# A planner that lets the accesses of all engines to one bank of products follow one another, reads too

## The chip, the cores and the metric

The kernel runs on one core of a Trainium2 chip. The core has a matmul engine (PE, with weight loads shown apart as PEld), a vector engine (DVE), an activation engine (ACT), GpSimd (POOL) and a queue that issues most transfers (SP). PE writes its products into eight banks of a memory of their own; DVE and ACT read them there. The metric is the device time of one execution in microseconds (us). The time before is the median of three runs: 1121.27 us (1120.59 to 1122.06).

## What is computed

One layer of a streaming encoder on 512 frames of 2048 features, all in float32:

```python
proj = einsum('btd,dc->btc', x, w_in)                  # 8320 columns
rw = token_shift(proj[..., :RWKV_COLS], shift_mu)      # y + mu * (y_prev - y)
o_rwkv = rwkv7_scan(...)                               # 16 heads of 64, gated with silu(z)
#   sa = S @ a_t;  S = S * w_t + sa b_t' + v_t k_t';  o_t = S @ r_t   for each frame
o_hgrn = hgrn2_chunkwise(...)                          # 8 heads of 128, gated
y = einsum('btc,cd->btd', concat([o_rwkv, o_hgrn]), w_out)
out = layer_norm(ALPHA * x + y) * ln_w + ln_b
```

## The kernel before, in words

**Projections.** Weights come in halves of 128 x 512 by `load` (SP, a ring of two tiles `wr`). `split` turns each into a rounded high part on ACT (`wh`, line 301) and a low part on DVE (`wl`, line 311); inputs are split in the same way into `xh` and `xl`. A product is then three wide matmuls of 512 columns (`three`, line 396). There are 65 blocks of 128 columns for the input projection, then the output projection in five column blocks. These wide matmuls fill a bank of the ring `main` (four banks); `shift`, `silu2` and `gates` drain it through ACT and DVE.

**Beside them** run the small works, as generators in queues: the preparation of a pair of RWKV heads (`rwkv_prep`), inversion and scan for two pairs at a time (`rwkv_group`, `rwkv_scan`), their end (`rwkv_finish`), and two HGRN heads at a time (`hgrn_heads`). There are four such groups, so four scan stretches. The scan goes chunk by chunk, eight chunks of 64 frames, and two pairs at once. In one chunk PE multiplies the state `bd` with `ar` into `px` (ring `acc`, two banks); DVE makes `rt` from it; PE makes `psa`; ACT or DVE copies that into `z`; PE multiplies `z` with `bt` into `pd` and puts the next chunk's share beside it in the same bank (ring `mix`, two banks). Out of `pd` DVE updates both halves of the state (line 320, `bd<-mix`), and the next `z` is copied (`z<-mix`, two halves of 64 x 64, ACT at line 301 or DVE at line 353). The other half of `px` is added to the output on DVE (line 311, `t<-t,acc`), which frees the bank.

**At the turn** from the input to the output projection, gated tiles that were put aside in DRAM (`put_gated`) come back through SP (`reload`, line 1184) and are split on ACT and DVE (`split_gated`). SP's queue holds them behind weight loads, and a weight load waits until the split of an older weight has freed its tile.

**Order.** Nothing is ordered by hand. While the kernel is built, a `Plan` keeps a clock for each engine. After each wide matmul, `pump` asks the head of each queue; `best` takes the engine on which the next operation would end first (a copy has a way on ACT and one on DVE), and `step` issues it if by the plan's clock its operands are there: PE only if they have been there for 0.35 us (`LEAD`), the others if they come within 0.5 us (`EARLY`). The start is worked out in `start` (line 79): each tile read must have been written (`seen`, which adds the hand-over `AFTER` from the writer's engine), and each tile written must be free of earlier accesses (`busy`), for PE only if the bank is newly taken. Two reads of one bank by two engines know nothing of one another there. On the chip each engine then works through its rows in the order in which they were issued, and waits on semaphores.

Of the kernel before, what the change touches and what calls it, by code (L numbers as in the profile page):

```python
# [56 lines left out]
class Plan:  # L57
# [11 lines left out]
    def __init__(self, room):  # L69
        self.clock = {"pe": 0.0, "dve": 0.0, "act": 0.0, "pool": 0.0, "dma": 0.0}  # L70
        self.table = None
        self.narrow = False
        self.queues = []
        self.ready, self.busy = {}, {}
        self.room = room
        self.slots = {tag: [(0, 0.0)] * n for tag, n in room.items()}
        self.count, self.used = 0, {}

    def start(self, e, op):

        t = 0.0
        for r in op.reads:
            t = max(t, self.seen(r, e))
        for w in op.writes:
            x, by = self.busy.get(w, (0.0, e))
            if e != "pe" or by is None:
                t = max(t, x if by == e else x + self.AFTER[by])
        return t

    def seen(self, name, e):  # L90

        x, by = self.ready.get(name, (-1.0, None))
        if by == e == "pe":
            return x
        return x + self.AFTER[by] + (self.TO_PE if e == "pe" else 0.0)
# [111 lines left out]
def mixer_kernel(ctx, tc, x_t, x_r, w_all, par, up, ln_wb, consts, hmask, out):  # L207
    nc = tc.nc
    pe, sc_e, dve, pool = nc.tensor, nc.scalar, nc.vector, nc.gpsimd
# [9 lines left out]
    def nm(s):  # L219
        uid[0] += 1  # L220
        return f"{s}{uid[0]}"
# [5 lines left out]
    plan = Plan({**BUFS, **PBUFS})  # L227
    tags = {}

    def st(tag, shape, dt=F32):  # L230
        return spool.tile(shape, dt, tag=tag, name=nm(tag), bufs=BUFS[tag])

    def take(tag, shape=(P, T), dt=F32):

        if not plan.free(tag):
            raise RuntimeError(f"no room: {tag}")
        slot = min(plan.slots[tag])
        plan.slots[tag].remove(slot)
        if tag in PBUFS:
            t = ppool.tile(list(shape), dt, tag=tag, name=nm(tag), bufs=PBUFS[tag])  # L240
        else:
            t = st(tag, list(shape), dt)
        name = t.tensor.name
        plan.busy[name] = (slot[1], None)
        tags[name] = tag
        return t
# [32 lines left out]
    def mm(o, l, r, start=True, stop=True, **kw):  # L279
        m, n = size(l), size(r)  # L280
        narrow = m < P or l.shape[0] < P
        if r.dtype == F32R:
            cost = n / 2400 + 0.0135
        elif narrow:
            cost = 0.025 if m <= 32 else 0.09 if m <= 64 else 0.16
        else:
            cost = n / 600 + 0.005
        return Op([("pe", cost, lambda: pe.matmul(o, l, r, start=start, stop=stop, **kw))], [l, r], [o],  # L288
                  narrow=narrow)
# [123 lines left out]
    def main_ps(tags=("main",)):  # L413

        def test():
            now = plan.clock["pe"]
            return [t for t in tags if plan.free(t) and min(plan.slots[t])[1] + 0.15 <= now]

        plan.until(test)
        return take(min(test(), key=lambda t: min(plan.slots[t])[1]))  # L420
# [110 lines left out]
    def shift(ps, col, put):  # L531
        def run():
            yield evac_room()
            t = take("t")
            yield act(t, ps, AF.Identity, scale=om[:, col : col + 1])
            yield stt(t[:, 1:], ps[:, : T - 1], pcol(PC_MU, col), t[:, 1:], ALU.mult, ALU.add)
            drop(ps)
            put(t)

        plan.add(evacs, run())  # L540
# [20 lines left out]
    def next_up():  # L561
        if len(ups) < NPAIR:
            upw = take("up", [P, 2, P])
            nc.sync.dma_start(upw, up[len(ups)])
            plan.fetched(upw, 8 * P)
            ups.append(upw)
# [810 lines left out]
    for b in range(4):  # L1377
        w = blocks[b][1]
# [88 lines left out]
```

## Time and profile before

| | |
|---|---|
| median of three runs | 1121.27 us |
| the profiled execution, its own time | 1123.09 us |
| its span, first to last instruction | 1121.3 us |
| granted TensorE clock, mean | 0.991 |
| last wide matmul starts | 1104.2 us |
| HBM read and written | 99.92 MB, 7.34 MB |

The span is what the trace covers. The scans stand in the stretches from about 140 to 220, 380 to 480, 580 to 660 and 830 to 930 us. The first output block begins at 916.6 us. A row of the timeline gives start, duration, engine, line, operation, the tiles written and read, and in brackets how long the engine was idle before it and who ended that.

### The profile page before, as it was taken

What the parts mean: (1) busy time and instruction counts of PE and PEld (TensorE: products, weight loads), DVE (VectorE), ACT (ScalarE), POOL (GpSimd) and SP (SyncE); (2) the same over time, 40 slices, a digit from 0 to 9 for tenths busy, and PEclk for the clock granted to TensorE, in tenths of its full rate; (3) what the DMA queues carried; (4) which work ended last, traced back from release to release, by engine and by line L of the source; (5) the groups of instructions that cost most, each with busy time, mean ns of one, the idle gap of its engine ahead of it and who ended that gap; (6) DMA issues with size and microseconds to landing.
All of it is one profiled execution on the core that took longest, in us unless ns stands there. A gap on an engine that the chain in (4) does not pass through costs nothing.

```text
span 1121.3 us, 19205 instructions
## 1 busy us (share of the span) xinstructions
PE 1091.5 (97%) x7402; PEld 901.8 (80%) x7402; DVE 766.5 (68%) x1739; ACT 456.3 (41%) x1042; POOL 88.6 (8%) x163
## 2 busy tenths in 40 slices
PE   8999999999999999999999999999999999999994
PEld 7878878788888878788887888888887778888893
DVE  6658967645579767857986774657976776624468
ACT  6532365433332465534245552433346444322221
POOL 0000000000010000101000010001000010000015
PEclk8999999999999999999999999999999999999997
DMA  7222211133323311223231122322231145433433
GB/s 274 85 80 93 95 59 58 57 99 94 90 75 103 96 58 59 67 79 117 76 104 58 58 76 87 99 92 77 94 102 46 52 141 194 136 122 110 144 126 138
DMA packets 36667, 108.50 MB, mean 97 GB/s; under 512 B 4320, under 2 KB 6496, under 8 KB 36448
## 3 DMA queue, kind: packets, MB, share of 16 engines
q1 hardware_dynamic: 34848, 104.33, 29.2%
q10 hardware_dynamic: 1728, 2.95, 0.7%
q8 instruction: 58, 0.95, 0.4%
q14 instruction: 33, 0.27, 0.1%
HBM read 99.92 MB, written 7.34 MB: 96 GB/s over the span
## 4 chain that ended last, share of the span: by engine, by line
PE 89%; DVE 6%; ACT 2%; issue 1%; DMA 1%; POOL 0%; SPq 0%; DVEq 0%; ACTq 0%
PE main L396 68%; PE mix L288 10%; PE mix L396 3%; PE acc L396 3%; PE acc L288 3%; PE mix L292 2%; DVE q L320 1%; DVE wl L311 1%; DVE t L311 1%; ACT z L301 1%; DVE bd L320 1%; ACT wh L301 1%; DMA t<-x_t 0%; DVE inv L320 0%; DMA t<-spill 0%
## 5 line engine op out<-in xcount | busy, mean ns | idle before, releaser
L396 PE MATMUL main<-xh,wh 128*128 128x512 f32 x896 | 358.0, 400 | 2.2 <-ACT xh L301 2.2
L396 PE MATMUL main<-xh,wl 128*128 128x512 f32 x896 | 356.6, 398 | 0.0
L396 PE MATMUL main<-xl,wh 128*128 128x512 f32 x896 | 356.0, 397 | 0.0
L301 ACT ACTIVATE wh<-wr 128x512 fp32r<-128x512 f32 (+1 forms) x313 | 195.5, 626 | 268.9 <-PE main L396 203.9
L311 DVE TENSOR_TENSOR wl<-wr,wh 128x512 fp32r<-128x512 f32 (+1 forms) x313 | 213.5, 683 | 130.2 <-ACT wh L301 126.9
L396 PEld LDWEIGHTS main<-xh,wh 128*128 128x128 f32 x896 | 169.1, 189 | 36.0 <-ACT xh L301 2.6
L396 PEld LDWEIGHTS main<-xl,wh 128*128 128x128 f32 x896 | 168.9, 188 | 33.8 <-DVE xl L311 0.8
L396 PEld LDWEIGHTS main<-xh,wl 128*128 128x128 f32 x896 | 168.9, 189 | 33.5
L396 PE MATMUL main<-wh,xh 128*128 128x512 f32 (+1 forms) x272 | 108.0, 397 | 1.9 <-DVE t L320 1.9
L396 PE MATMUL main<-wh,xl 128*128 128x512 f32 (+1 forms) x272 | 108.1, 397 | 0.0
L396 PE MATMUL main<-wl,xh 128*128 128x512 f32 (+1 forms) x272 | 107.4, 395 | 0.0
L301 ACT ACTIVATE z<-mix 64x64 f32<-64x64 f32 (+1 forms) x245 | 56.0, 229 | 92.1 <-DVE bd L320 71.4
L396 PEld LDWEIGHTS main<-wh,xh 128*128 128x128 f32 x272 | 51.3, 189 | 10.4 <-DVE t L320 2.3
L396 PEld LDWEIGHTS main<-wh,xl 128*128 128x128 f32 x272 | 51.3, 189 | 8.6
L396 PEld LDWEIGHTS main<-wl,xh 128*128 128x128 f32 x272 | 51.3, 189 | 8.2
L302 ACT ACTIVATE t<-main,om 128x512 f32<-128x512 f32 x33 | 22.6, 688 | 61.2 <-PE main L396 61.1
L320 DVE SCALAR_TENSOR_TENSOR bd<-mix,pc,bd 64x64 f32<-64x64 f32 x112 | 31.2, 283 | 22.4 <-PE mix L288 17.2
L343 POOL TENSOR_TENSOR rs<-rs,mhalf 128x8 f32<-128x8 f32 (+1 forms) x16 | 25.1, 1572 | 250.3 <-DVE rs L316 129.5
L311 DVE TENSOR_TENSOR inv<-inv 64x30 f32<-64x30 f32 (+14 forms) x120 | 38.6, 322 | 3.1
L311 DVE TENSOR_TENSOR inv<-inv,inv 64x30 f32<-64x30 f32 (+14 forms) x120 | 38.6, 322 | 2.9
L346 POOL MEMSET z<- 64x128 f32 x64 | 11.9, 199 | 355.7 <-PE acc L288 312.1
L311 DVE TENSOR_TENSOR t<-t,tot 128x256 f32<-128x256 f32 x96 | 38.4, 416 | 0.2
(207 smaller groups left out, 1489.1 us busy)
## 6 DMA issues: line engine op xcount, KB each, us to landing
wr<-w_all SPq DMA_DIRECT2D x158, 512.0 KB, 3.5
t<-x_t SPq DMA_DIRECT2D x16, 256.0 KB, 5.6
g<-x_r SPq DMA_DIRECT2D x16, 256.0 KB, 4.2
spill<-g SPq DMA_DIRECT2D x12, 256.0 KB, 4.3
t<-spill SPq DMA_DIRECT2D x12, 256.0 KB, 4.0
big<-ln_wb SPq DMA_DIRECT2D x1, 2048.0 KB, 9.1
out<-q ACTq DMA_DIRECT2D x7, 256.0 KB, 2.4
up<-up SPq DMA_DIRECT2D x8, 128.0 KB, 2.8
```

What stands on the lines that cost most here:

```text
L288: return Op([("pe", cost, lambda: pe.matmul(o, l, r, start=start, stop=stop, **kw))], [l, r], [o], narrow=narrow)
L292: return Op([("pe", 0.11, lambda: pe.transpose(o, i, ident))], [i], [o])
L301: return "act", cost, lambda: sc_e.activation(o, i, f, scale=scale)
L302: return "act", cost, lambda: sc_e.activation(o, i, f, scale=scale, bias=bias)
L311: return dve_op([a, b], o, lambda: dve.tensor_tensor(o, a, b, f), base=0.16 if o.shape[0] < P and size(o) == C and o.tensor.name in tags e ...
L320: return dve_op([a, b], o, lambda: dve.scalar_tensor_tensor(o, a, s, b, f1, f2), per=0.00113, base=0.085 if o.shape[0] == P else 0.25 if s ...
L343: lambda: pool.tensor_tensor(o, i, mhalf[:, : size(o)], ALU.pow))], [i], [o])
L346: return Op([("pool", 0.1, lambda: pool.memset(o, v))], [], [o])
L396: pe.matmul(ps, l, r, start=first and i == 0, stop=last and i == 2)
```

## The change

A tile from one of the rings of banks is entered in a set `banks`. A read of such a tile now also waits, in the plan, for the last access of any other engine to it, be it a write or a read (`done`). A write by PE now waits for another engine's last access to the bank; between PE's own accesses there is still no wait. Nothing else in the kernel changes: the same operations with the same shapes, their order and the choice between ACT and DVE being the plan's.

```diff
-        self.ready, self.busy = {}, {}
+        self.ready, self.busy, self.banks = {}, {}, set()
...
         for r in op.reads:
             t = max(t, self.seen(r, e))
+            if r in self.banks:
+                t = max(t, self.done(r, e))
         for w in op.writes:
-            x, by = self.busy.get(w, (0.0, e))
-            if e != "pe" or by is None:
-                t = max(t, x if by == e else x + self.AFTER[by])
+            t = max(t, self.done(w, e))
         return t
+
+    def done(self, name, e):
+
+        x, by = self.busy.get(name, (0.0, e))
+        return (0.0 if e == "pe" else x) if by == e else x + self.AFTER[by]
...
             t = ppool.tile(list(shape), dt, tag=tag, name=nm(tag), bufs=PBUFS[tag])
+            plan.banks.add(t.tensor.name)
```

What this moves, in two places. Line numbers after the change are 5 or 6 higher (L301 becomes L307, L311 L317, L320 L326, L353 L359).

*First place: the second scan stretch, a chunk in its middle.* `bd` is the state, `z` the next chunk's input, and both are read out of one bank (`mix_4269` of the one pair and `mix_4275` of the other before, `mix_4312` and `mix_4424` now). DVE before:

```order
L320 SCALAR_TENSOR_TENSOR bd_3736<-mix_4269,pc_3088,bd_3736 64x64
L320 SCALAR_TENSOR_TENSOR bd_3719<-mix_4275,pc_2695,bd_3719 64x64
L320 SCALAR_TENSOR_TENSOR bd_3736<-mix_4269,pc_3088,bd_3736 64x64
L311 TENSOR_TENSOR wl_4285<-wr_4103,wh_4284 128x512
L320 SCALAR_TENSOR_TENSOR bd_3719<-mix_4275,pc_2695,bd_3719 64x64
L311 TENSOR_TENSOR t_2762<-t_2762,acc_4222 64x64
```

DVE now:

```order
L326 SCALAR_TENSOR_TENSOR bd_3735<-mix_4312,pc_3088,bd_3735 64x64
L333 COPY_PREDICATED nr_3908<-hm,mix_4317 128x8x8
L333 COPY_PREDICATED nr_3909<-hm,mix_4317 128x8x8
L317 TENSOR_TENSOR t_3449<-t_3449,tot_3910 128x32x8
L326 SCALAR_TENSOR_TENSOR rt_3720<-acc_4307,z_3715 64x128
L326 SCALAR_TENSOR_TENSOR bd_3735<-mix_4312,pc_3088,bd_3735 64x64
L317 TENSOR_TENSOR wl_4359<-wr_4081,wh_4358 128x512
L359 COPY z_3732<-mix_4312 64x64 x2
```

ACT at the same place before:

```order
L301 ACTIVATE t_3160<-acc_4212 64x128
L301 ACTIVATE t_2762<-acc_4222 64x128
L301 ACTIVATE z_3733<-mix_4269 64x64 x2
L301 ACTIVATE wh_4284<-wr_4103 128x512
L301 ACTIVATE z_3713<-mix_4275 64x64 x2
L301 ACTIVATE bd_3718<-bd_3719,pc_2695 128x128
```

ACT now:

```order
L307 ACTIVATE wh_4407<-wr_4213 128x512
L307 ACTIVATE bd_3736<-bd_3735,pc_3088 128x128
L307 ACTIVATE z_3730<-mix_4416 64x128
L307 ACTIVATE z_3731<-mix_4416 64x128
L307 ACTIVATE bt_3733<-mix_4416 128x128
L307 ACTIVATE t_3160<-acc_4402 64x128
L307 ACTIVATE z_3732<-mix_4436 64x64 x2
L307 ACTIVATE z_3713<-mix_4424 64x64
```

The copy of `z` from the bank of the one pair has gone from ACT to DVE, behind DVE's own two reads of that bank; of the other pair's copy one half stays on ACT, later in its queue. The two chunks no longer interleave as tightly.

*Second place: the turn to the output projection, on DVE.* `xl` is the low part of the first reloaded tile. Before, from the split that frees the tile for SP's next weight load:

```order
L311 TENSOR_TENSOR wl_9119<-wr_8893,wh_9118 128x512
L353 COPY z_8255<-mix_9133 64x64 x2
L317 TENSOR_SCALAR sm_9041<-sm_9041 128x8
L353 COPY t_9025<-nr_8430 32x4x32
L320 SCALAR_TENSOR_TENSOR t_9147<-main_8911,pr,t_9147 128x511
L311 TENSOR_TENSOR wl_9160<-wr_9005,wh_9159 128x512
L311 TENSOR_TENSOR t_7683<-t_7683,acc_9107 64x64 x2
L311 TENSOR_TENSOR t_7287<-t_7287,sm_9041 128x512
L311 TENSOR_TENSOR xl_9178<-t_9138,xh_9177 128x512
```

Now the same split (`wl_9086`) stands seven rows above the first of these:

```order
L317 TENSOR_TENSOR t_7972<-t_7972,tot_8433 128x8x32
L317 TENSOR_TENSOR t_8068<-t_8068,tot_8433 128x8x32
L317 TENSOR_TENSOR tot_8434<-tot_8433 128x8
L317 TENSOR_TENSOR t_8182<-t_8182,tot_8435 128x8x32
L317 TENSOR_TENSOR t_8404<-t_8404,tot_8435 128x8x32
L317 TENSOR_TENSOR t_7287<-t_7287,acc_9076 64x64
L317 TENSOR_TENSOR tot_8436<-tot_8435 128x8
L317 TENSOR_TENSOR wl_9157<-wr_9018,wh_9156 128x512
L317 TENSOR_TENSOR t_7287<-t_7287,acc_9076 64x64
L326 SCALAR_TENSOR_TENSOR bd_8258<-mix_9188,pc_7611,bd_8258 64x64
L330 TENSOR_REDUCE sm_9173<-t_7287 128x8
L317 TENSOR_TENSOR xl_9199<-t_9108,xh_9198 128x512
```

Seventeen rows instead of seven lie between the two; HGRN rows (`tot`) that came later before now stand here, and the last scan chunk still runs here. In the whole program the wide matmuls keep their order; the scans end up to 35 wide matmuls later in each stretch, and 53 instructions go from ACT to DVE.

## The prediction

> **What bounds the kernel now.** I read the head of the page first, then the table of busy time by stretches, then the starts on PE one by one, then the waits.
>
> ```profile
> span 1121.3 us, 19205 instructions
> PE 1091.5 (97%) x7402; PEld 901.8 (80%) x7402; DVE 766.5 (68%) x1739; ACT 456.3 (41%) x1042; POOL 88.6 (8%) x163
> ```
>
> PE holds 97% of the span and nobody else comes near, so the time is PE's work plus the moments in which PE starts late. The change leaves PE's 7402 matmuls as they are. What it can win or lose is lateness, and the table by stretches says where that is:
>
> ```profile
> 140.00:220.00 80.00, 78.16 (x882) 63.99 (x872) 56.63 (x186) 45.18 (x146) 4.94 (x13) 1.00 0.17 55
> 220.00:380.00 160.00, 160.00 (x836) 131.30 (x835) 106.95 (x199) 56.70 (x95) 11.26 (x20) 1.00 0.30 94
> 380.00:480.00 100.00, 97.86 (x934) 79.38 (x933) 75.55 (x219) 53.60 (x159) 6.37 (x15) 1.00 0.21 66
> 480.00:580.00 100.00, 100.00 (x492) 82.64 (x491) 78.48 (x153) 35.68 (x61) 7.81 (x18) 1.00 0.31 93
> 580.00:660.00 80.00, 78.78 (x874) 64.54 (x873) 54.49 (x175) 42.84 (x140) 6.38 (x13) 1.00 0.21 65
> 660.00:830.00 170.00, 169.99 (x893) 139.20 (x892) 113.04 (x218) 60.78 (x104) 11.25 (x20) 1.00 0.30 91
> 830.00:930.00 100.00, 95.35 (x887) 77.13 (x886) 71.83 (x209) 52.02 (x155) 7.39 (x14) 1.00 0.27 85
> 930.00:1100.00 170.00, 170.00 (x954) 148.35 (x953) 89.73 (x158) 46.69 (x80) 14.48 (x14) 1.00 0.42 138
> ```
>
> The columns are the stretch, its length, then PE, weight loads, DVE, ACT and POOL busy, the granted clock, DMA. PE idles in the four stretches in which the recurrent scans run (1.84, 2.14, 1.22 and 4.65 us, 9.85 together) and not at all between them. The clock is 1.00 in all, so it explains nothing.
>
> Busy time hides part of a late start, because a matmul is shown longer than the time to the next start. So I took the distances between starts:
>
> ```profile
> 153.00 0.39 PE L288 MATMUL acc<-z,big 128*128 128x128 f32 x2
> 153.22 0.39 PE L288 MATMUL mix<-z,big 128*128 128x128 f32 x2
> ...
> 154.58 0.40 PE L396 MATMUL main<-wl,xh 128*128 128x512 f32 x1
> 154.81 0.40 PE L396 MATMUL main<-wh,xl 128*128 128x512 f32 x1
> ...
> 155.27 0.40 PE L396 MATMUL main<-wl,xh 128*128 128x512 f32 x1
> 155.60 0.89 PE L288 MATMUL mix<-q,t 128*32 128x48 f32 x64
> 156.42 0.50 PE L396 MATMUL main<-wh,xl 128*128 128x512 f32 x1
> 156.76 0.38 PE L288 MATMUL acc<-bd,q 128*128 128x128 f32 x2
> ...
> 157.21 0.27 PE L292 MATMUL mix<-cst,t 128*128 128x128 f32 x1
> 157.61 0.46 PE L288 MATMUL acc<-bd,q 128*128 128x128 f32 x2
> ```
>
> ```profile
> 923.68 0.40 PE L396 MATMUL main<-wh,xh 128*128 128x512 f32 x1
> 924.45 0.41 PE L292 MATMUL mix<-cst,t 128*128 128x128 f32 x2 [0.37 <-DVE t L311]
> ```
>
> A wide matmul is followed after 0.23 us, a pass of 128 columns after 0.11 (two in 0.22). From 140 to 930 us, 31 starts come more than 0.12 us after that; the first (157.61, 0.40 instead of 0.11) and the last (924.45, 0.77 instead of 0.23) are shown. Their sum is **15.2 us**. The table agrees: 9.85 idle plus 31 times 0.17 hidden (0.40 shown, 0.23 real) is 15.1. Twenty-nine stand beside the scans (12.6 us), two at the turn to the output projection (2.6 us). That is all that any new order can win.
>
> What makes them late? One stretch, read downwards:
>
> ```profile
> 429.80 0.58 DVE L320 SCALAR_TENSOR_TENSOR bd<-mix,pc,bd 64x64 f32<-64x64 f32 x2 [0.62 <-PE mix L288]
> 430.47 0.45 ACT L301 ACTIVATE z<-mix 64x64 f32<-64x64 f32 x2 [3.09 <-DVE bd L320]
> 430.83 0.62 ACT L301 ACTIVATE wh<-wr 128x512 fp32r<-128x512 f32 x1
> 431.48 0.69 DVE L311 TENSOR_TENSOR wl<-wr,wh 128x512 fp32r<-128x512 f32 x1 [1.10 <-ACT wh L301]
> ...
> 432.57 0.45 ACT L301 ACTIVATE z<-mix 64x64 f32<-64x64 f32 x2 [1.13 <-DVE bd L320]
> ...
> 433.01 0.40 PE L396 MATMUL main<-xl,wh 128*128 128x512 f32 x1
> 433.44 0.47 DVE L311 TENSOR_TENSOR t<-t,acc 64x64 f32<-64x64 f32 x2
> 433.81 0.46 PE L288 MATMUL acc<-bd,q 128*128 128x128 f32 x2 [0.40 <-DVE t L311]
> ```
>
> ACT stands for 3.09 us at a copy out of a bank that DVE is also reading. It needs nothing that DVE makes: both only read. Behind it in ACT's queue is the weight split wh; DVE's wl waits 1.10 for that, DVE's next rows come late, and PE starts 0.57 late (0.80 instead of 0.23) because the accumulator slot isn't drained. The list of waits has this pair as a group:
>
> ```profile
> ACT z L301 <- DVE bd L320: 71.4, 44, 3.1
> ```
>
> I followed eight of the 29 back, at least one of each kind of waiter (acc, mix, rt); each led to such a wait of one reader for another of the same bank. The planner's book has no such wait, so it put rows behind it that were ready in its book and not in fact.
>
> **The change, part by part.** Same-bank reads now wait in the plan too, and PE's writes wait for readers. *Removed*: the rows that stand too early. The new order of DVE and ACT at this spot (shown above) has the one head's copy on DVE, behind DVE's two reads, and half of the other head's; on ACT the split wh no longer stands behind a copy that has to wait for both. *Added*: work on DVE, off ACT.
>
> ```profile
> L301 ACT ACTIVATE z<-mix x245: 204/221/275, 146.4 to 902.8; 64x64 f32<-64x64 f32 x101, 64x128 f32<-64x128 f32 x22
> L353 DVE COPY z<-mix x75: 205/226/296, 145.8 to 905.8; 64x64 f32<-64x64 f32 x54, 64x128 f32<-64x128 f32 x21
> ```
>
> In the new order these are 179 on ACT and 141 on DVE. In all 53 instructions go over net, some 12 us of DVE at 0.226 each. It lies beside PE: DVE is busy 258.5 of the 360 us of the four stretches (72%), and 12 more make 75%. If that cover fails it costs what the slower rival below says.
>
> *Lateness beside the scans*: bounds are 0 (like the stretches between) and 12.6 or more (a new order can be late elsewhere). The nearest rows for a plan that knows its waits are those between the scans, with 0.01 us idle in 430 us under the same planner. I don't take 0, since the hand-overs themselves remain and DVE is fuller: I leave a quarter, 3.0. **Won: 9.6 us.**
>
> *Turn to the output projection*:
>
> ```profile
> 906.15 2.50 SPq L1184 DMA_DIRECT2D t<-spill  x5
> 910.89 0.63 ACT L301 ACTIVATE xh<-t 128x512 fp32r<-128x512 f32 x1 [3.94 <-DMA t<-spill]
> 911.56 0.69 DVE L311 TENSOR_TENSOR xl<-t,xh 128x512 fp32r<-128x512 f32 x1 [2.53 <-ACT xh L301]
> ...
> 918.48 0.63 ACT L302 ACTIVATE ksq<-t 128x512 f32<-128x512 f32 x1 [3.82 <-DVE t L311]
> 919.01 0.67 ACT L302 ACTIVATE t<-main,om 128x512 f32<-128x512 f32 x1
> 920.68 0.50 PE L396 MATMUL main<-wh,xh 128*128 128x512 f32 x1 [1.92 <-DVE t L320]
> ```
>
> The first reload leaves SP at 906.15 (SP's queue stood at a weight load until the split freed its slot) and lands 4.7 us later. ACT waits 3.94, DVE 2.53 with it. DVE then runs behind, ACT's ksq waits for it, the drain of the last projection comes after that, and PE stands 2.1 us for the bank (1.92 and the hidden 0.17), then 0.5 at 924.45. In the new order seventeen DVE rows stand between the split that frees the slot and the first reloaded tile, instead of seven. Ten more at 0.22 or over (half of the x2 row at 433.44) are 2.2 us at least, about the 2.53 that DVE stood. SP's own order is the same there: the load, then five reloads. But 33 DVE rows, not 18, now lie between the drains of the last two projections. Bounds: 2.6 won, or 2.4 lost (12 us over four stretches, one share of which falls here). I take 2.0, as the idle of 2.53 is what the new rows fill. **Won: 2.0 us.**
>
> *PE's own sequence*: groups of narrow matmuls between wide ones are 322 instead of 319. A group costs two switches, 0.33 and 0.34 where a wide one takes 0.23 (155.27 to 155.60, 156.42 to 156.76): 0.21 in all, three of them **0.6 lost**. *Later scans*: the last accumulator product of the last scan stands behind 3108 wide matmuls, not 3080, 28 times 0.23 or 6.4 us later; PE does other wide ones meanwhile, and the last gated tiles are first read at the end of block 0, some 180 wide matmuls (41 us) on. Nothing.
>
> A rule against the change: the Trainium skill (PSUM — Partial Sum Buffer, "PSUM bank collisions raise a hardware error") bars two engines from one bank only within one quadrant of 32 partitions, reads included, and allows different quadrants at once. By that, ACT's copy of the upper half could have gone after the first of the two DVE reads and the new plan would be stricter than the chip. The trace disagrees for this program: ACT's copy starts at 430.47, after the second read (the x2 row of 429.80 ends at 430.38). If waits were by quadrant, perhaps half of the 9.6 would be lost to needless caution, and the sum 1115.1.
>
> Sum: 1121.3 - 9.6 - 2.0 + 0.6 = **1110.3** for the span. The profiled execution took 1123.09, 1.8 more than its span; the median of the runs, 1121.27, is 1.8 under it. Both cancel: 1110.3.
>
> **Rivals.** (a) *The lateness is only halved*, because DVE, fuller, takes over part of ACT's role: for it speaks that DVE already waits for wh and drains accumulators itself; against it that most z copies now sit behind DVE's own reads. Half of 12.6 and nothing at the turn: 1121.3 - 6.3 + 0.6 = 1115.6; with less, up to 1119. (b) *It doesn't do what it says*: the waits are there in the hardware order whatever the plan knows, and new rows come late in their place. Time 1121.3 + 0.6 = about 1121.9. Against: the clean stretches between scans. (c) *Slower*: 66 z copies sit in DVE's queue, where a copy that waits for PE holds the weight split wl and the accumulator drains behind it. A late accumulator drain costs PE 0.57 at 433.81, say 0.5 each. With ACT's 12.6 gone and 0.6 added, it decides from 24 such copies of 66 (12.0 us); at 36 it is 1121.3 - 12.0 + 18.0 = 1127.3. Against: in the trace these copies take 0.226 and come right after a read of the same bank, which had to wait for the same product.
>
> **How the numbers follow.** Forecast (1106 to 1115): 0.62. Rival (a), 1115 to 1119: 0.21. Rival (b), 1119 to 1123.5: 0.10. Rival (c), above: 0.07. All 15.2 gone would be 1106.1, the lower end. From there to 1118 lies the forecast and most of (a), 0.80. A measurement of this kernel can tell about 0.2% (2.2 us) from no change: faster than that (under 1119) 0.83, within it 0.10, slower 0.07.
>
> **What would show it.** Right: the group of ACT's z waiting for DVE's bd shrinks from 71.4 us to under 20; PE idle in the four stretches falls from 9.85 to under 3; the drain of the last projection isn't waited for over 1 us; DVE's busy time up by some 10 us, ACT's down. Rival (a) or (c): DVE z or DVE wl appear as releasers of PE. Rival (b): ACT's waits go and PE's idle time stays. The forecast is wrong if PE turns out late between the scans too.

## The result, and the profile after

The changed kernel takes **1101.95 us** (median of four runs, 1101.89 to 1103.25) against 1120.93 for the one before in runs on the same chip: a ratio of 0.9832, interval 0.9815 to 0.9849, or 19.0 us less. Forecast were 1110.3, with 1106 to 1118 as the range. The sign and the mechanism were right, the size was little more than half of what came, and the time lies below the range. The profiled execution took 1101.89 us, its span 1100.1.

The head of the page of the changed kernel, and the shares of its chain of work by engine (the chain is followed back from the last instruction, at each step to what released it):

```profile
span 1100.1 us, 19128 instructions
PE 1080.4 (98%) x7402; PEld 902.9 (82%) x7402; DVE 776.9 (71%) x1792; ACT 447.6 (41%) x989; POOL 86.2 (8%) x163
...
PE 96%; DVE 3%; DMA 0%; issue 0%; SPq 0%; DVEq 0%; ACT 0%
```

The same line before:

```profile
PE 89%; DVE 6%; ACT 2%; issue 1%; DMA 1%; POOL 0%; SPq 0%; DVEq 0%; ACTq 0%
```

PE was 89% of the chain before and is 96% now: hardly anything but PE's own work is left on the way to the end. The same is seen in the stretches of the scans (columns as before: stretch, length, PE, weight loads, DVE, ACT, POOL, clock, DMA):

```profile
140.00:220.00 80.00, 80.00 (x851) 68.21 (x850) 61.66 (x205) 41.78 (x130) 4.56 (x13) 1.00 0.20 62
...
380.00:480.00 100.00, 100.00 (x895) 83.65 (x894) 79.05 (x233) 51.08 (x141) 7.32 (x16) 1.00 0.20 66
...
580.00:660.00 80.00, 80.00 (x782) 67.95 (x781) 61.49 (x203) 39.85 (x122) 5.13 (x13) 1.00 0.22 67
...
830.00:930.00 100.00, 100.00 (x886) 84.74 (x886) 80.27 (x226) 53.11 (x145) 8.70 (x14) 1.00 0.31 101
```

PE idled 9.85 us in these four and idles 0.00 now, with DVE busier in each of them; these are the same stretches of time, but not quite the same pieces of the program. The list of waits (total, times, longest), and the groups of the z copies:

```profile
ACT z L307 <- DVE bd L326: 10.8, 9, 1.6
```

```profile
L307 ACT ACTIVATE z<-mix 64x64 f32<-64x64 f32 (+1 forms) x179 | 41.9, 235 | 62.1 <-PE mix L298 30.4 <-PE mix L294 18.2 <-DVE bd L326 10.8
L359 DVE COPY z<-mix 64x64 f32<-64x64 f32 (+1 forms) x141 | 31.8, 226 | 13.2 <-PE mix L294 11.0 <-PE mix L298 0.3
```

The wait of ACT for DVE went from 71.4 us in 44 waits to 10.8 in 9. ACT's z copies still have 62.1 us of idle time before them, but most of it is now time in which PE hasn't yet made the product. A chunk in the second scan stretch, near the place where ACT stood 3.09 us before; DVE first, then ACT:

```profile
423.52 0.29 DVE L326 SCALAR_TENSOR_TENSOR bd<-mix,pc,bd 64x64 f32<-64x64 f32 x1
423.85 0.69 DVE L317 TENSOR_TENSOR wl<-wr,wh 128x512 fp32r<-128x512 f32 x1
424.57 0.46 DVE L359 COPY z<-mix 64x64 f32<-64x64 f32 x2
425.04 0.21 DVE L317 TENSOR_TENSOR t<-t,acc 64x64 f32<-64x64 f32 x1
...
425.94 0.46 ACT L307 ACTIVATE z<-mix 64x64 f32<-64x64 f32 x2
426.31 0.62 ACT L307 ACTIVATE wh<-wr 128x512 fp32r<-128x512 f32 x1
```

None of these rows has a bracket: neither engine stood idle before them. ACT copies z without having stood for it, and the split wh goes right behind.

**Where the time went.** I cut both traces at the same wide matmuls (the n-th of 4080), since the same moment in us is another place in the program. From there to there the first scan's part takes 104.09 us before and 100.08 now, the second's 120.02 and 116.52, the third's 110.75 and 107.67, the fourth's 82.10 and 78.50, the turn 43.36 and 39.33, and the rest of the output projection 144.78 both times. Together that is **18.2 us**. The fourth scan and the turn are to be taken together: 44 narrow matmuls that stood behind the cut between them stand before it now. The first 140 us differ by 3.0 more between these two profiled executions, ahead of the first changed row (near 144 us), so that part isn't the change. The stretch from 10 to 20 us, before and then after, shows it in the last column but two, the granted clock:

```profile
10.00:20.00 10.00, 10.00 (x33) 7.96 (x34) 9.25 (x14) 8.05 (x14) 0.00 (x0) 0.72 1.05 394
10.00:20.00 10.00, 10.00 (x46) 8.26 (x45) 8.46 (x13) 8.16 (x14) 0.00 (x0) 1.00 1.05 395
```

The execution that was profiled before had 0.72 there and PE came to 33 matmuls, the one after 1.00 and 46. It is why the spans differ by 21.2, more than the 19.0 of the medians.

### The profile page after: what moved, and what is told of

Same layout as the page of the kernel before. It is cut to its first block, busy times and chain, and to the rows that moved or that the text cites. A ratio compares the mean times of both kernels' runs of the same rounds, so it can differ in the third digit from the quotient of the medians.

```text
span 1100.1 us, 19128 instructions
## 1 busy us (share of the span) xinstructions
PE 1080.4 (98%) x7402; PEld 902.9 (82%) x7402; DVE 776.9 (71%) x1792; ACT 447.6 (41%) x989; POOL 86.2 (8%) x163
## 4 chain that ended last, share of the span: by engine, by line
PE 96%; DVE 3%; DMA 0%; issue 0%; SPq 0%; DVEq 0%; ACT 0%
PE main L402 74%; PE mix L294 11%; PE mix L402 3%; PE acc L402 3%; PE mix L298 2%; PE acc L294 2%; DVE q L326 1%; DVE inv L326 0%; DMA t<-x_t 0%; DVE stats L1342 0%; SPq L1086 0%; DVE xl L317 0%; DVE mv L1285 0%; DVE q L339 0%; DVE mv L322 0%
## 5 line engine op out<-in xcount | busy, mean ns | idle before, releaser
L307 ACT ACTIVATE wh<-wr 128x512 fp32r<-128x512 f32 (+1 forms) x313 | 195.5, 626 | 269.9 <-PE main L402 207.0
L317 DVE TENSOR_TENSOR wl<-wr,wh 128x512 fp32r<-128x512 f32 (+1 forms) x313 | 213.5, 683 | 115.6 <-ACT wh L307 112.8
L307 ACT ACTIVATE z<-mix 64x64 f32<-64x64 f32 (+1 forms) x179 | 41.9, 235 | 62.1 <-PE mix L298 30.4
L326 DVE SCALAR_TENSOR_TENSOR bd<-mix,pc,bd 64x64 f32<-64x64 f32 x112 | 31.7, 283 | 25.2 <-PE mix L294 20.8
L359 DVE COPY z<-mix 64x64 f32<-64x64 f32 (+1 forms) x141 | 31.8, 226 | 13.2 <-PE mix L294 11.0
L317 DVE TENSOR_TENSOR inv<-inv 64x30 f32<-64x30 f32 (+14 forms) x120 | 38.7, 322 | 3.1
L317 DVE TENSOR_TENSOR inv<-inv,inv 64x30 f32<-64x30 f32 (+14 forms) x120 | 38.7, 322 | 2.9
L352 POOL MEMSET z<- 64x128 f32 x64 | 11.9, 199 | 355.2 <-PE acc L294 311.7
```

The lines of the kernel that those rows point to most:

```text
L307: return "act", cost, lambda: sc_e.activation(o, i, f, scale=scale)
L317: return dve_op([a, b], o, lambda: dve.tensor_tensor(o, a, b, f), base=0.16 if o.shape[0] < P and size(o) == C and o.tensor.name in tags e ...
L326: return dve_op([a, b], o, lambda: dve.scalar_tensor_tensor(o, a, s, b, f1, f2), per=0.00113, base=0.085 if o.shape[0] == P else 0.25 if s ...
L352: return Op([("pool", 0.1, lambda: pool.memset(o, v))], [], [o])
L359: f = lambda: dve.tensor_copy(o, i)
```

## The experiments

Four theories were set against each other:
- **A**: the book's blindness. It isn't the waits themselves that cost, but rows that the plan puts behind a wait it doesn't know.
- **B**: slack. Any larger caution of the plan toward PE would give the same.
- **C**: the choice of engine. What counts is that z copies left ACT.
- **D**: the order of before was an unlucky one, and nearly any other would be better.

In the table, "late" is the sum (and the number) of PE's starts from 140 us on that come over 0.12 us later than usual after the row before them; one of 0.16 us that all these kernels have isn't counted. What is usual is here taken from both kernels' traces, which makes 15.3 of the prediction's 15.2 and 32 starts of its 31. Each ratio is to the kernel before on the same chip as the run (1120.4 to 1120.9 us). "Wait" is ACT's z waiting for DVE's bd, from the list of waits of each run.

| run | edit | median, us | ratio to before (95%) | late, us | wait, us |
|---|---|---|---|---|---|
| before | | 1120.93 | | 15.3 (32) | 71.4 |
| after | | 1101.95 | 0.9832 (0.9815 to 0.9849) | 0 | 10.8 |
| x1_lead_cautious | blind, LEAD -0.8 | 1106.82 | 0.9876 (0.9861 to 0.9891) | 2.3 (5) | 68.0 |
| x2_z_on_dve | blind, z from pd on DVE | 1106.36 | 0.9870 (0.9856 to 0.9885) | 2.0 (3) | 0 |
| x3_after_z_on_act | knowing, z from pd on ACT | 1103.76 | 0.9847 (0.9832 to 0.9861) | 0.7 (1) | 47.2 |
| x4_pd_only | only pd's banks known | 1106.61 | 0.9873 (0.9857 to 0.9890) | 2.1 (3) | 26.9 |
| y1_not_pd | all banks but pd's known | 1107.49 | 0.9882 (0.9867 to 0.9897) | 5.0 (11) | 48.5 |
| y2_early0 | blind, EARLY 0 | 1115.02 | 0.9948 (0.9933 to 0.9963) | 10.7 (31) | 54.0 |
| y3_after_lead_small | knowing, LEAD -0.1 | 1105.43 | 0.9864 (0.9847 to 0.9880) | 1.7 (10) | 19.6 |
| y4_after_lead_large | knowing, LEAD -0.8 | 1104.25 | 0.9853 (0.9838 to 0.9868) | 0.4 (1) | 15.2 |
| z1_before_lead_small | blind, LEAD -0.1 | 1118.28 | 0.9975 (0.9966 to 0.9985) | 11.0 (31) | 50.4 |
| z2_before_nudge_act | blind, ACT's hand-over 0.16 | 1114.21 | 0.9944 (0.9927 to 0.9960) | 7.8 (22) | 56.8 |
| z3_after_nudge_act | knowing, ACT's hand-over 0.16 | 1102.31 | 0.9837 (0.9822 to 0.9852) | 0 | 15.0 |
| z4_before_nudge_pe | blind, hand-over to PE 0.14 | 1121.44 | 1.0009 (1.0000 to 1.0019) | 14.5 (32) | 72.3 |

"Blind" is the planner of before, "knowing" the changed one.

### Does the wait itself cost? (x2, x3)

x2 takes the z copies of `pd` off ACT in the blind planner; x3 puts all of them on ACT in the knowing one.

```diff
                 for h in range(2):
-                    yield copy(zs[(c + 1) % 3][0:64, hc[h]], block(pd, h, P))
+                    op = copy(zs[(c + 1) % 3][0:64, hc[h]], block(pd, h, P))
+                    op.ways = op.ways[1:]     # x2: DVE alone; x3: [:1], ACT alone
+                    yield op
```

> The kernel before, with the copies of z out of pd on DVE alone, so that DVE alone reads that bank; the plan stays blind. Theory A: the group of ACT z waiting for DVE bd goes to nearly nothing, other reads of one bank by ACT and DVE (turned chunks, HGRN scores) still wait unplanned, 3 to 6 us of late starts are left: 1104 to 1109. Rival C (the gain is the choice of engine, no hand-over between readers): 1101 to 1103, all of it. If neither the bank nor the choice matters: 1119 to 1122.

> The changed kernel, with the copies of z out of pd on ACT alone: every one is a hand-over from DVE's reads, but the plan knows the wait. Theory A: no row stands before its time, PE's late starts stay under 1 us in sum, 1101 to 1104. Rival C (choice of engine): the hand-overs are back and with them 10 to 16 us, 1112 to 1118.

x3 is the run that tells most. Its list of waits, and its stretches:

```profile
ACT z L307 <- DVE bd L326: 47.2, 29, 3.1
```

```profile
140.00:220.00 80.00, 80.00 (x852) 68.13 (x851) 58.20 (x193) 43.97 (x143) 4.46 (x13) 1.00 0.19 61
380.00:480.00 100.00, 100.00 (x905) 83.66 (x904) 79.14 (x228) 52.76 (x151) 8.91 (x16) 1.00 0.21 68
580.00:660.00 80.00, 80.00 (x782) 67.80 (x781) 58.45 (x193) 42.38 (x133) 4.84 (x13) 1.00 0.21 67
830.00:930.00 100.00, 99.46 (x884) 83.78 (x883) 78.59 (x219) 54.69 (x154) 8.86 (x14) 1.00 0.30 96
```

ACT again stands 47 us for DVE's reads, up to 3.1 us at a time as before, and PE idles 0.54 us where it idled 9.85. The waits are there and cost next to nothing, as A expects of waits that the plan knows. It takes C away: with every such copy on ACT the time is 1103.76, 17 us better than before. x2 is the other side: with no such wait left in a blind plan, 14.4 of the 19 us are won. That is inside A's range, with fewer late starts than A asked for (2.0 us for 3 to 6), and it doesn't reach the changed kernel. But both runs also have new orders, and whether any new order would do as well is asked below.

### Caution instead of knowledge (x1, y2, y3, y4)

```diff
-    LEAD = -0.35
+    LEAD = -0.8        # x1 in the blind planner, y4 in the knowing one; y3: -0.1, knowing
...
-    EARLY = 0.5
+    EARLY = 0.0        # y2, blind
```

> The kernel before, with LEAD -0.8 in place of -0.35: PE's rows are issued 0.45 us later against their operands, and the plan stays blind to reads of one bank by two engines. Theory A (the plan put rows of ACT and DVE behind a wait that it did not know): the waits of ACT z for DVE bd stay above 40 us; of the 31 late starts those over 0.45 us keep a rest, and time falls only in part, to 1106 to 1115. Rival B (any plan that is more cautious gains as much): PE's lateness goes as it did after the change, 1101 to 1104.

> The kernel before, with EARLY 0 in place of 0.5: ACT and DVE take a row only when its operands are there by the plan; the plan stays blind to reads of one bank. Theory A: the unknown wait is 1 to 3 us long and can't be avoided by 0.5 us less haste: 1112 to 1121, ACT z waits for DVE bd above 40 us. Rival B (haste in the queues of ACT and DVE is the cause): 1101 to 1107.

> The changed kernel, with LEAD -0.1 in place of -0.35: PE's rows may stand 0.25 us nearer to their operands. Theory A (the plan's book is right now): late starts under 3 us in sum, 1101 to 1105. Rival B (a margin of caution is what protects PE, in the old plan as in the new): late starts above 6 us, 1108 to 1116.

> The changed kernel, with LEAD -0.8: more caution where PE is never late. Theory A: nothing is left to win, 1101 to 1103.5, late starts under 0.5 us. If caution and knowledge add up: under 1100.

x1's list of waits shows a plan as blind as before:

```profile
ACT z L301 <- DVE bd L320: 68.0, 42, 4.5
```

Yet 14 of the 19 us are won, and the late starts go to 2.3 us: PE is given narrow work only when its operands have been there for 0.8 us by the plan's clock, and most of what comes late by the unknown waits fits into that. Read so, the unknown waits cost time only where what comes late by them exceeds the slack that PE is given; no run tests that reading by itself. Caution for the other engines (y2) wins 5.4, inside A's range. So B holds in large part, and x1 lies at the low end of what A allowed (1106 to 1115); but it stops short of the changed kernel (1106.82), and with the knowing book the same caution no longer helps: y4 is 2.3 us slower than the changed kernel, and y3, with far less caution than before, keeps 15 of the 19. y3 and y4 both came out slightly above what A expected of them (0.4 and 0.75 us).

### Which banks? (x4, y1)

```diff
-            plan.banks.add(t.tensor.name)                # x4: not for every tile of a ring of banks
...
                 pd = take("mix")
+                plan.banks.add(pd.tensor.name)           # x4; y1 instead: discard, with the line above kept
```

> The changed kernel, with only pd's banks known to the plan (state update and next z), not the other banks of the ring mix. Theory A, with pd as the costly bank (44 waits, 71 us): 1102 to 1106, late starts under 4 us in sum. If the other banks of the ring (turned chunks, psa, HGRN scores) cost as much: 1108 to 1114.

> The complement of the run with pd's banks alone: all banks of the ring mix known to the plan except pd's. Theory A with pd as the costly bank: the convoys stay, PE's late starts 7 to 13 us in sum, 1112 to 1118. If the gains of the two halves add up (14.2 us with pd alone of 18.8): 4.6 us, 1116. If either half does (any disturbance of the old order helps): 1105 to 1108.

The lists of waits of x4, then of y1:

```profile
ACT z L306 <- DVE bd L325: 26.9, 18, 3.8
```

```profile
ACT z L307 <- DVE bd L326: 48.5, 33, 2.9
```

Both missed A's first range: x4 is 0.6 us above it, y1 4.5 us below, with 5.0 us of late starts for 7 to 13. y1 lies where it was to lie if any disturbance of the old order helps (1105 to 1108). To know only the bank of `pd` wins 14.2 us, to know all but that one wins 12.9, both together 19.0 (each against the kernel before on its own chip). The halves don't add up: either changes the whole order that comes after. My picture, in which the pair z and bd carries nearly all, was too narrow. I had followed only eight late starts back; by these two runs the other products in the same ring (`nr`, `bt`, `t` read by DVE and ACT) can be as much a part of it. How much of y1's gain is theirs, and how much any new order's, the two don't tell.

Two things are seen from the orders alone, row for row on all engines: the new rule for reads without the new rule for PE's writes gives exactly the order of the changed kernel, and the rule for writes alone gives exactly that of before. And to enter only the ring `mix` in `banks` gives the changed order too. So the change is its read rule, on one ring of two banks; the other parts do nothing here.

### Was the order of before an unlucky one? (z1 to z4)

x1, x2, x4 and y1 all ended near 1107, which is what D says: disturb the order in some way, and most of the gain comes. So here the blind planner gets disturbances that tell it nothing of reads, and two of them stand as pairs to a knowing one.

```diff
-    LEAD = -0.35
+    LEAD = -0.1                                  # z1, blind: the pair of y3
...
-    AFTER = {"pe": 0.2, "act": 0.145, "dve": 0.13, "pool": 0.06, "dma": 0.0, None: 0.1}
+    AFTER = {"pe": 0.2, "act": 0.16, "dve": 0.13, "pool": 0.06, "dma": 0.0, None: 0.1}   # z2, blind; z3, knowing
...
-    TO_PE = 0.12
+    TO_PE = 0.14                                 # z4, blind
```

> The planner of before with less caution for PE (LEAD -0.1 instead of -0.35), the pair of the run of the changed kernel with that caution, which took 1105.4 us; only the book differs between the two. Theory A (a book that misses the waits between readers costs PE late starts whatever the caution): 1114 to 1124 us, with ACT's z waiting for DVE's bd 55 us or more and over 9 us of late starts on PE. Rival D (the order of before is only an unlucky one, and any other order that a blind book gives would be about as good as the new ones): 1104 to 1111 us.

> The planner of before with a number that has no bearing on the change nudged: the hand-over from ACT is priced at 0.16 us instead of 0.145. Almost all rows move, the book stays blind. Theory A: 1114 to 1124 us, ACT's z waiting for DVE's bd 55 us or more. Rival D (before is a bad draw): 1104 to 1111 us.

> The changed planner with the same nudge (hand-over from ACT 0.16 us instead of 0.145): the pair of the run before. Theory A: 1101 to 1106 us, late starts under 2.5 us. Rival D (the gain is a matter of which order comes out): it lies as far from 1102 as chance has it, no better than the blind one with the nudge.

> The planner of before with another small nudge: the further hand-over to PE is priced at 0.14 us instead of 0.12, which moves fewer rows. Theory A: 1115 to 1124 us, ACT's z waiting for DVE's bd 60 us or more. Rival D: 1104 to 1112 us.

The stretches of the pair with the nudged hand-over, blind (z2) and then knowing (z3):

```profile
140.00:220.00 80.00, 79.19 (x837) 65.31 (x836) 58.04 (x189) 44.61 (x146) 4.56 (x13) 1.00 0.19 61
380.00:480.00 100.00, 98.84 (x885) 80.93 (x884) 75.50 (x224) 52.29 (x154) 8.67 (x16) 1.00 0.20 63
580.00:660.00 80.00, 78.54 (x825) 64.03 (x824) 58.12 (x188) 40.06 (x131) 5.09 (x13) 1.00 0.18 55
830.00:930.00 100.00, 99.47 (x874) 82.03 (x873) 76.77 (x223) 52.99 (x158) 6.85 (x14) 1.00 0.28 93
```

```profile
140.00:220.00 80.00, 80.00 (x852) 68.23 (x851) 59.99 (x196) 45.43 (x143) 4.56 (x13) 1.00 0.21 65
380.00:480.00 100.00, 100.00 (x894) 83.77 (x893) 79.22 (x234) 51.34 (x142) 6.73 (x15) 1.00 0.21 66
580.00:660.00 80.00, 80.00 (x781) 67.86 (x780) 61.35 (x204) 39.90 (x122) 4.69 (x13) 1.00 0.22 67
830.00:930.00 100.00, 100.00 (x878) 84.58 (x877) 79.34 (x227) 51.47 (x141) 7.46 (x13) 1.00 0.35 115
```

| setting | blind, us | knowing, us | difference |
|---|---|---|---|
| LEAD -0.1 (z1, y3) | 1118.28 | 1105.43 | 12.9 |
| LEAD -0.35 (before, after) | 1120.93 | 1101.95 | 19.0 |
| the same, ACT's hand-over 0.16 (z2, z3) | 1114.21 | 1102.31 | 11.9 |
| LEAD -0.8 (x1, y4) | 1106.82 | 1104.25 | 2.6 |

The times fell as A has it, though z1 had a little less of the wait than A asked for (50.4 us for 55). Blind orders of the same operations, with PE's caution as before or less, lie between 1114 and 1121.5, knowing ones between 1102 and 1105.5. D falls as the main cause; it keeps a part. A neutral nudge of one number moved the blind plan by 6.2 us against the kernel before on the same chip (z2) or by nothing that can be told apart (z4). At PE's caution of before or less, all three pairs give the knowledge 11.9 us or more, so **some 12 of the 19 us belong to the knowledge, and up to 7 to the order that happened to be there before**. Three pairs are few, and with LEAD -0.8 the knowledge is worth 2.6 us: most of what it wins, caution can win too. No run beat the changed kernel; z3 equals it within the measurement.

x2 and x4 are some 4.5 us above the changed kernel with only 2 us of late starts. From the same wide matmul at 140 us to the last one, the traces have 948.6 and 949.2 us where the changed kernel has 945.2. In x4, late starts and those right after them are 2.2 of the 4.0; 1.3 are the usual distances of another sequence on PE, and 0.6 are starts under 0.12 us late. In x2 the three are 2.2, -0.5 and 1.8. Another 0.9 and 0.8 us lie in the first 40 us of these profiled executions, ahead of the scans.

What stays open: which rows make one blind order 7 us better than another wasn't followed.

## Why the prediction was right in its mechanism and wrong in its size

By medians, 19.0 us were won where the sum had 11.0. Step by step:

- **What bounds the kernel: held.** PE's lateness was all that moved; its work took the same time within 0.1 us.
- **Why PE is late: held.** ACT's wait shrank to 10.8 us (forecast under 20), PE's idle time to 0.00 (under 3), DVE's busy time rose by 10.4 and ACT's fell by 8.7; x3 shows that the wait alone doesn't cost it, and the pairs of blind and knowing plans that the ignorance does (11.9 to 19.0 us). What I left out is the slack: x1 keeps 68 us of such waits in a blind plan, and PE is late by 2.3 us.
- **Lateness beside the scans: the step that failed.** I had 12.6 us there, took 9.6 and left a quarter, 3.0, "since the hand-overs themselves remain and DVE is fuller". Nothing of it was left: no start is over 0.12 us late, and all 12.6 us were won. The nearest row that I had quoted (0.01 us idle in 430 us between the scans, under the same planner) gave the right answer, and I shaded it without a row that spoke for a remainder. DVE did get fuller, to 282.5 of the 360 us of the same stretches of time (78%, from 72%), and PE was never late for it. The other knowing orders leave 0 to 1.7 us of late starts (z3, x3, y4, y3), all under my 3.0; that this one leaves nothing at all may be luck.
- **"That is all that any new order can win": wrong.** The 15.2 us counted only the late starts themselves. After nearly all of them the next start is late too, mostly by 0.07 to 0.11 us, below my bound of 0.12; the 31 followers make about 2.5 us. The section on the hardware shows two.
- **Turn: right, sized 0.6 short** (2.0 of 2.6). The cover of DVE rows held. The bound of 2.4 us lost there is a slip, since 12 us over four stretches are 3.0; it entered no sum. The timeline of the changed kernel there, SP, ACT and DVE:

```profile
884.23 0.33 SPq L382 DMA_DIRECT2D wr<-w_all  x1
884.65 2.47 SPq L1190 DMA_DIRECT2D t<-spill  x5
...
890.55 0.62 ACT L307 ACTIVATE xh<-t 128x512 fp32r<-128x512 f32 x1
...
891.41 0.67 DVE L317 TENSOR_TENSOR xl<-t,xh 128x512 fp32r<-128x512 f32 x1
```

  The reload leaves SP at 884.65, and neither ACT's xh 5.9 us later nor DVE's xl has a wait before it, where they had 3.94 and 2.53. PE doesn't wait at the turn at all.
- **PE's own sequence: 0.6 charged, 0 found.** There are 322 groups of narrow matmuls instead of 319, but the usual distances of all starts, added up, agree within 0.1 us.
- **Later scans: nothing, as said.** The output projection takes 144.78 us both times.

The four sizes make 3.0 + 2.5 + 0.6 + 0.6 = 6.7 of the 8.0 us that were missing. Some 0.5 lies in starts under 0.12 us late; the other 0.8 lies between the medians (19.0) and the profiled stages (18.2).

Of the rivals, halved lateness (1115.6) and no effect (1121.9) didn't come; they are what blind plans with other numbers look like (z2, z4). The slower one didn't either: 141 z copies stand on DVE, and PE never waits for one of them or for a wl. As to the rule of the Trainium skill (PSUM — Partial Sum Buffer, "PSUM bank collisions raise a hardware error"): the sum by quadrants, 1115.1, had half of the gain beside the scans lost to needless caution, and nothing of the kind is seen: the plan that treats whole banks leaves PE without a late start. No run here has a plan that goes by quadrants.

The range was too narrow for the same reason as the sum: its lower end, 1106, was the 15.2 us taken as a bound of what can be won.

## What to carry to other kernels

The length of a wait says little about its price; what counts is what the plan put behind it, and with how much slack. Here 71 us of waits that the plan didn't know went with 12 to 19 us of lost time, 68 us unknown with under 5 when PE had more slack (x1), and 47 us that it knew with under 2 (x3). Look for waits between two readers in a kernel whose plan tracks writers alone, and if the plan's rule can't be corrected, more slack toward the engine that bounds the kernel gets most of it. And before a change of a planner's rule is credited with its whole gain, nudge a number that doesn't matter: here that alone moved the time by up to 6 of 19 us.

## What the hardware showed beyond that

A late start on PE cost more than its own delay here. Two places in the kernel before, first PE's matmuls and then, for the second place, the weight loads (PEld) beside them:

```profile
167.43 0.39 PE L396 MATMUL main<-wh,xl 128*128 128x512 f32 x1
168.12 0.49 PE L288 MATMUL acc<-bd,q 128*128 128x128 f32 x2 [0.31 <-DVE t L311]
168.45 0.27 PE L292 MATMUL mix<-cst,q 128*128 128x128 f32 x1
...
920.68 0.50 PE L396 MATMUL main<-wh,xh 128*128 128x512 f32 x1 [1.92 <-DVE t L320]
921.02 0.40 PE L396 MATMUL main<-wl,xh 128*128 128x512 f32 x1
921.26 0.39 PE L396 MATMUL main<-wh,xl 128*128 128x512 f32 x1
```

```profile
920.68 0.19 PEld L396 LDWEIGHTS main<-wh,xh 128*128 128x128 f32 x1 [2.34 <-DVE t L320]
920.79 0.19 PEld L396 LDWEIGHTS main<-wl,xh 128*128 128x128 f32 x1
921.02 0.19 PEld L396 LDWEIGHTS main<-wh,xl 128*128 128x128 f32 x1
```

The two passes of 168.12 take 0.33 us to the next start instead of 0.22, and the wide one of 920.68 takes 0.34 instead of 0.23. In the running sequence the load for a matmul starts one step ahead of it (921.02 for the one of 921.26); after the stop load and matmul are both shown at 920.68, and the next load comes at 920.79. So the load for the next matmul starts 0.11 us after the stopped matmul instead of together with it, and the start behind it is late by as much. Over 31 stops it was about 2.5 us, a sixth on top of the lateness that I had counted.
